# A two-layer backbone kernel: branch products between gate streams, modulation in single matmuls, casts on another engine

## The chip, the cores and the metric

The kernel runs on one core of a Trainium2 chip. The metric is the device time of one execution in microseconds (us), as the median of several runs. The engines are TensorE (PE, with its weight loads listed as PEld), VectorE (DVE), ScalarE (ACT), GpSimd (POOL) and SyncE (SP), which issues the DMAs.

## What is computed

The reference is a backbone of two layers over 512 latent tokens and 256 context tokens of width 1024, in float32. Each layer modulates its normalised input, mixes tokens, passes an MLP, and adds the residual. Cut to the part that the change touches:

```python
mod_l = (silu_c @ w_mod[i] + b_mod[i])           # six sections of 1024: shift, scale, gate, twice
hl = _modulate(xl, sh1_l, sc1_l)
ul_pool, ul_q, ul_k, ul_v, ul_conv, ul_gate = _split_in(hl @ w_in[i] + b_in[i])
ol = _latent_attention(ql, kl, vl, kc, vc, attn_sink[i])     # 8 query heads, 2 key/value heads
# _merge:
y_pool = _pool_mixer(u_pool, pool_w, pool_scale) @ w_pool_out
y_attn = o_attn @ w_attn_out
y_conv = _conv_module(u_conv, conv_w, conv_b, conv_ln_g, conv_ln_b, w_conv_out)
g_pool, g_attn, g_conv = jnp.split(jax.nn.sigmoid(gates), N_BRANCH, axis=-1)
return (g_pool * y_pool + g_attn * y_attn + g_conv * y_conv) @ w_out
```

Context tokens go through the same in layer 0; in layer 1 they serve as keys and values only. The modulation sections 3 and 4 (second shift and scale) of layer 0 are wanted by layer 0's MLP; section 2 is the first gate.

## The kernel before

Float32 products are made of three float32r matmuls each: every operand is split into a high part (a cast to float32r) and a low part (the rest). Weights come by DMA as `raw` tiles of 128x512, ACT casts the high part (L134), POOL or DVE subtracts for the low part (L137), and `mm_a_steps` (L156) issues high x high, high x low and low x high. Where tokens are the moving operand, a stream is 512 columns (latent, LS) or 256 columns (context, CS).

A layer has two phases. `w_phase` makes the input projection, the three mixers, the gates and the branch products; `m_phase` makes the output projection (L165 to L167), the MLP and the next layer's first projections. PE's order is the program's order, written by hand with generators: `drain` runs steps and calls `tick` with each step's columns; `tick` starts tasks that are due (attention blocks, put off by a number of columns with `later`) and, every so many columns, takes one step of a paced generator (`pace`). The instructions of the other engines are ordered by a scheduler, which starts from the program's order.

In `w_phase`, `gated_steps` is the work that covers waits: first the eight attention gates (type 1), then for each of eight output tiles m the pool gate (0) with its branch product and the conv gate (2) with its own. `cover(n)` takes n columns of it while the convolution runs on DVE and while the conv normalisation passes between engines; in the attention stage it is taken step by step between attention tasks. A branch product may be issued only once its input is `mixed`; until then the generator yields None and `cover` returns. `gate_steps` makes one gate: per stream 24 matmuls into a PSUM bank of `psg` (two banks), then a Tanh on ACT (L611). `branch_steps` makes a branch product of 6 matmuls per stream (12 in the last loop) and lets DVE multiply it with the gate (L621). During attention these products take their banks from `psa` (two banks), which the attention's value products (L451, L452) and the conv normalisation use too; afterwards they take them from `psg`.

`mod_steps` makes one modulation section with plain float32 matmuls of a 128x32 stationary operand (L185): for each of eight k, four matmuls with 256 columns each that write to the partitions 0, 32, 64 and 96 of one bank; each matmul is two instructions. In layer 0, section 2 is paced from the start of the phase; sections 3 and 4 are paced from the end of attention on, every 9000 columns, with weight tiles of 512 KB, and what is left of them is issued behind the last branch product (the loop before `pace(None, 0)`).

Queries: `query` evacuates a projection (L665), rotates it (`rope`, L406 to L409), and splits it for each head pair with a cast on DVE (L676) and a subtraction on DVE (L677). Keys: a cast on DVE (L710), a copy on ACT (L711) and two subtractions on DVE (L713) for each of two heads. The second group's queries are made in the middle of the attention.

Of the kernel before, what the change touches and what calls it, by code (L numbers as in the profile page):

```python
# [10 lines left out]
F32 = mybir.dt.float32  # L11
F32R = mybir.dt.float32r
# [6 lines left out]
P = 128  # L19
# [46 lines left out]
ON_C = "G"  # L66
MODVC = ()
W_VAL = 9000
W_CONV0 = 145000
W_CONV1 = 118000  # L70
T_POOL, T_Q, T_K, T_V, T_A, T_B, T_G = 0, 2, 6, 7, 8, 10, 12
# [6 lines left out]
def backbone(ctx: ExitStack, tc: tile.TileContext, I: dict, out: bass.AP):  # L78
# [10 lines left out]
    def uid(s):  # L89
        cnt["n"] += 1  # L90
        return f"{s}_{cnt['n']}"
# [31 lines left out]
    def weight_unit(ap):  # L123
        with tc.high_priority(ring["early"]):
            return weight_parts(ap)
# [47 lines left out]
    def mod_steps(i, s, c0, n, chunk, psum=None, ps=None, row=None):  # L173


        q = n // 4
        ps = bank(psum) if ps is None else ps
        for k in range(KD):
            for j in range(4):
                if j == 0 or (j * q) % w.shape[-1] == 0:  # L180
                    w = chunk()
                    c = c0 + j * q
                    nc.sync.dma_start(out=w, in_=I["wmod"][i, s, k, :, c:c + w.shape[-1]])
                o = (j * q) % w.shape[-1]
                T.matmul(ps[32 * j:32 * j + 32, :q], sc[:, k, :], w[:, o:o + q],  # L185
                         start=(k == 0), stop=(k == KD - 1))
            yield
        mod_finish(i, s, c0, n, ps, row)
        yield
# [221 lines left out]
    def softmax_pv(pp, pss, g, Pt, vtiles, negm, sums, V_, sink, dst, qsl):  # L411
# [26 lines left out]
        for n0 in range(0, nt, 2):  # L438
# [12 lines left out]
                T.matmul(po, w, ph, start=(n == 0), stop=False)  # L451
                T.matmul(po, w, pl, start=False, stop=(n == nt - 1))  # L452
            yield 1024 * len(ns), W_PV
        t1 = pp.tile([64, 4, P], F32, tag="t1", name=uid("t1"), bufs=1)
        S.copy(t1, po[64:128, :].rearrange("p (a q) -> p a q", a=4))
        ot = pp.tile([P, 2, P], F32, tag="ot", name=uid("ot"), bufs=2)
        top = po[0:64, :].rearrange("p (a q) -> p a q", a=4)
        for par in range(2):
            V.tensor_add(ot[64 * par:64 * par + 64, :, :], top[:, par::2, :], t1[:, par::2, :])
# [91 lines left out]
    def pace(steps, every, start=0):  # L551
        pe["pace"], pe["every"], pe["next"] = steps, every, pe["t"] + start
# [7 lines left out]
    def w_phase(i, A, B, has_ctx, pre, todo):  # L560
# [5 lines left out]
        with ExitStack() as ph:  # L566
# [24 lines left out]
            psg = ph.enter_context(tc.tile_pool(name=f"psg{i}", bufs=2, space=PSUM, reuse_waits="tile"))  # L591
            pss = mix.enter_context(tc.tile_pool(name=f"pss{i}", bufs=2, space=PSUM, reuse_waits="tile"))
            if todo:
                pace((x for s in todo for x in mod_steps(i, s, 0, D, lambda: mg.tile(
                    [P, W], F32, tag="sg", name=uid("wm"))[:, :512])), 10000, 20000)

            def proj(t, sls):
# [2 lines left out]
                drain(mm_a_steps(w, A, range(KD), o))  # L600
                return [x[0] for x in o]

            def gate_steps(m, b):

                t = KD * b + m
                w = weight_a(I["win"][i, T_G + t])
                g = mg.tile([P, W], F32, tag="sg", name=uid("sg"))
                for _, sl in outs_all:
                    ps = bank(psg)[:, :sl.stop - sl.start]
                    yield from mm_a_steps(w, A, range(KD), [(ps, sl)])  # L610
                    S.activation(g[:, sl], ps, AF.Tanh, bias=bg[:, t:t + 1], scale=0.5)  # L611
                return g

            def branch_steps(w, ks, w0, g, outs, pool):

                while ks[0] not in mixed:
                    yield None
                for _, sl in outs:
                    ps = bank(pool)[:, :sl.stop - sl.start]
                    yield from mm_a_steps(w, B, ks, [(ps, sl)], w0)  # L620
                    V.scalar_tensor_tensor(out=g[:, sl], in0=g[:, sl], scalar=1.0, in1=ps,  # L621
                                           op0=ALU.add, op1=ALU.mult)

            def gated_steps():
                for m in range(KD):
                    g = yield from gate_steps(m, 1)
                    nc.sync.dma_start(out=sgd[m], in_=g)

                w, d, e, ahead = {}, {}, {}, 0 if todo else 2
                for m in range(ahead):  # L630
                    d[m] = yield from gate_steps(m, 0)
                for m in range(KD + 1):
                    if m + ahead < KD:
                        d[m + ahead] = yield from gate_steps(m + ahead, 0)
                    if m < KD:
                        w[m] = weight_a(I["wbr"][i, m][:, 0:4 * P])
                        yield from branch_steps(w[m], (0, 1), 0, d[m], outs_all, side["bank"])
                    if m:
                        e = yield from gate_steps(m - 1, 2)
                        yield from branch_steps(w.pop(m - 1), (2, 3), 2, e, outs_all, side["bank"])  # L640
                        G.tensor_tensor(out=d[m - 1], in0=d[m - 1], in1=e, op=ALU.add)
                        nc.sync.dma_start(out=mfd[m - 1], in_=d.pop(m - 1))

            mixed, side = set(), {"bank": psa}
            other = gated_steps()

            def cover(cols):
# [20 lines left out]
            def query(Q, g, jj, temp):  # L668
                t = T_Q + 2 * g + jj
                qf = evac(proj(t, LC), t)  # L670
                rope(temp, qf, cs)
                for par in range(2):
                    r = slice(64 * par, 64 * par + 64)
                    ro = slice(64 - 64 * par, 128 - 64 * par)
                    q = Q[2 * jj + par]
                    V.tensor_copy(q[r, :W], qf[r, :W])  # L676
                    V.tensor_tensor(out=q[ro, :W], in0=qf[r, :W], in1=q[r, :W].bitcast(F32),  # L677
                                    op=ALU.subtract)

# [139 lines left out]
            ring["on"] = "GV"  # L819

            fin = ph.enter_context(tc.tile_pool(name=f"fin{i}", bufs=3, reuse_waits="tile"))
            side["bank"] = psg
            if todo:
                pace((x for s in (3, 4) for x in mod_steps(i, s, 0, D, lambda: fin.tile(
                    [P, D], F32, tag="wm", name=uid("wm"), bufs=4))), 9000)
            drain(other)
            for m in range(KD):
                w = weight_a(I["wbr"][i, m][:, 4 * P:8 * P])
# [5 lines left out]
                V.tensor_add(d, d, g)  # L834
                split(A[0][:, m, :W], A[1][:, m, :W], d[:, :], S, G)
            if todo:
                for _ in pe["pace"]:
                    pass
            pace(None, 0)

# [228 lines left out]
    with tc.manual_schedule(engines={mybir.EngineType.PE}):  # L1069
# [159 lines left out]
```

## Time and profile before

| | |
|---|---|
| median of 3 runs | 1978.15 us (1974.14 to 1978.68) |
| profiled execution | 1975.67 us, span from first to last instruction 1973.9 us |
| PE busy | 1848.6 us, 94% of the span |
| DVE, ACT, POOL busy | 1200.3 us (61%), 730.8 us (37%), 771.6 us (39%) |
| mean granted TensorE clock | 0.978 |
| DMA | 244.94 MB, mean 124 GB/s |

Busy time of an engine is the union of its instructions' spans. A row of the timeline gives start, duration, engine, line, operation, operands, and, in brackets, idle time before it with what ended that idle time. Matmuls are pipelined: the time that one takes from its neighbours is read from start to start, not from its duration. In layer 0, `w_phase` runs from about 60 to 543 us of the span, its attention from about 243 to 477; in layer 1 the attention lies at about 1353 to 1527.

### The profile page before, as it was taken

The numbers are of one execution on the slowest core, as the hardware profiler recorded it, in microseconds if no ns is written. First come the engines' busy times: TensorE is split into PE (matmuls) and PEld (weight loads), VectorE is DVE, ScalarE is ACT, GpSimd is POOL, SyncE is SP. The second block draws the span as 40 slices with busy tenths as digits, with TensorE's granted clock in tenths as the row PEclk, the third lists the DMA queues.
The fourth block names the chain that finished last, engine by engine and source line by source line (L and its number), as shares of the span: only waits on it lengthen the run. The fifth ranks groups of instructions, "written<-read, shape, count | busy, mean of one in ns | idle before, by whom it ended". The sixth has DMA issues, their size and how long they took to land. (4 is left out here: it accounts for less than half of the span.)

```text
span 1973.9 us, 27007 instructions
## 1 busy us (share of the span) xinstructions
PE 1848.6 (94%) x9910; PEld 1548.4 (78%) x9910; DVE 1200.3 (61%) x2067; ACT 730.8 (37%) x1359; POOL 771.6 (39%) x629
## 2 busy tenths in 40 slices
PE   6999899899899999999999988999988989999997
PEld 4788788787678888888788868777866768888886
DVE  6489655654478946865533584786575784333356
ACT  4432255353234422233133344434444354333331
POOL 3653432322434422222122546664342554333343
PEclk8999999999999999999999989999999989999999
DMA  8523111114865434464422423141212753332341
GB/s 304 176 90 118 62 59 46 53 44 154 281 219 190 161 112 133 155 213 143 146 62 86 129 96 105 61 149 63 69 65 96 260 189 118 96 96 86 107 129 43
DMA packets 117557, 244.94 MB, mean 124 GB/s; under 512 B 14608, under 2 KB 16944, under 8 KB 117424
## 3 DMA queue, kind: packets, MB, share of 16 engines
q1 hardware_dynamic: 117424, 243.21, 38.0%
q8 instruction: 78, 1.28, 0.3%
q14 instruction: 55, 0.45, 0.1%
HBM read 223.20 MB, written 19.96 MB: 123 GB/s over the span
## 5 line engine op out<-in xcount | busy, mean ns | idle before, releaser
L137 POOL TENSOR_TENSOR wl<-raw,wh 128x512 fp32r<-128x512 f32 x371 | 516.7, 1405 | 783.6 <-ACT wh L134 698.9
L134 ACT CAST wh<-raw 128x512 fp32r<-128x512 f32 x506 | 310.8, 621 | 596.0 <-PE ps L167 292.1
L156 PE MATMUL ps<-actbh,wh 128*128 128x512 f32 (+1 forms) x1016 | 353.4, 348 | 14.3 <-DVE sg L621 6.9
L156 PE MATMUL ps<-actbl,wh 128*128 128x512 f32 (+1 forms) x1016 | 348.3, 343 | 3.1 <-POOL actbl L251 3.1
L156 PE MATMUL ps<-actbh,wl 128*128 128x512 f32 (+1 forms) x1016 | 347.8, 342 | 2.7 <-DVE rs L261 1.3
L156 PE MATMUL ps<-actah,wh 128*128 128x512 f32 (+1 forms) x928 | 331.4, 357 | 13.7 <-ACT actah L248 4.7
L156 PE MATMUL ps<-actal,wh 128*128 128x512 f32 (+1 forms) x928 | 327.4, 353 | 3.3 <-DVE actal L1097 1.9
L156 PE MATMUL ps<-actah,wl 128*128 128x512 f32 (+1 forms) x928 | 326.9, 352 | 0.4 <-POOL wl L137 0.3
L156 PEld LDWEIGHTS ps<-actbh,wh 128*128 128x128 f32 x1016 | 194.5, 191 | 45.2 <-DVE sg L621 10.0
L156 PEld LDWEIGHTS ps<-actbh,wl 128*128 128x128 f32 x1016 | 194.4, 191 | 25.6 <-DVE wl L137 2.4
L156 PEld LDWEIGHTS ps<-actbl,wh 128*128 128x128 f32 x1016 | 194.6, 192 | 23.3 <-POOL actbl L251 3.8
L156 PEld LDWEIGHTS ps<-actah,wh 128*128 128x128 f32 x928 | 177.5, 191 | 43.8 <-ACT actah L248 5.1
L156 PEld LDWEIGHTS ps<-actal,wh 128*128 128x128 f32 x928 | 177.6, 191 | 25.6 <-DVE actal L1097 2.2
L156 PEld LDWEIGHTS ps<-actah,wl 128*128 128x128 f32 x928 | 177.4, 191 | 24.2 <-POOL wl L137 1.0
L165 PE MATMUL ps<-wh,actah 128*128 128x512 f32 x480 | 192.6, 401 | 2.2 <-DVE acc L977 2.0
L167 PE MATMUL ps<-wh,actal 128*128 128x512 f32 x480 | 190.5, 397 | 3.5 <-DVE actal L251 3.5
L166 PE MATMUL ps<-wl,actah 128*128 128x512 f32 x480 | 190.1, 396 | 0.0
L137 DVE TENSOR_TENSOR wl<-raw,wh 128x512 fp32r<-128x512 f32 x135 | 127.8, 947 | 99.9 <-ACT wh L134 97.3
L204 DVE SCALAR_TENSOR_TENSOR wm<-wm,sc,wm 128x512 f32<-128x512 f32 x140 | 124.4, 924 | 67.1 <-DMA wm<-in_wmod 67.0
L970 DVE TENSOR_TENSOR acc<-ps,acc 128x512 f32<-128x512 f32 x140 | 94.7, 684 | 95.3 <-PE ps L167 95.2
L165 PE MATMUL ps<-wh,actbh 128*128 128x512 f32 (+1 forms) x328 | 127.2, 388 | 1.5 <-DVE fg L621 1.5
L166 PE MATMUL ps<-wl,actbh 128*128 128x512 f32 (+1 forms) x328 | 126.8, 387 | 1.0 <-POOL wl L137 1.0
(207 smaller groups left out, 2721.7 us busy)
## 6 DMA issues: line engine op xcount, KB each, us to landing
raw<-in_w SPq DMA_DIRECT2D x264, 256.0 KB
raw<-in_win SPq DMA_DIRECT2D x154, 256.0 KB
wm<-in_wmod SPq DMA_DIRECT2D x72, 512.0 KB
raw<-in_wout SPq DMA_DIRECT2D x56, 256.0 KB
wm<-in_wmod SPq DMA_DIRECT2D x48, 256.0 KB
raw<-in_wbr SPq DMA_DIRECT2D x32, 256.0 KB
x1d<-R SPq DMA_DIRECT2D x10, 512.0 KB
acc<-in_b SPq DMA_DIRECT2D x10, 512.0 KB
```

Of the source, the lines that this page charges most:

```text
L134: S.copy(wh, r)
L137: e.tensor_tensor(out=wl, in0=r, in1=wh[:].bitcast(F32), op=ALU.subtract)
L156: T.matmul(ps, w(hl, w0 + n), x[xi][:, k, sl], start=(start and first and hl == 0 and xi == 0), stop=(stop and last and hl == 1))
L165: T.matmul(ps, x[0][:, k0 + k, tsl], wh, start=(k == 0), stop=False)
L166: T.matmul(ps, x[0][:, k0 + k, tsl], wl, start=False, stop=False)
L167: T.matmul(ps, x[1][:, k0 + k, tsl], wh, start=False, stop=(k == n - 1))
L204: V.scalar_tensor_tensor(out=o, in0=x, scalar=sc[:, k, r:r + 1], in1=o, op0=ALU.mult, op1=ALU.add)
L970: V.tensor_add(a, ps, a)
```

## The change

- Branch products are no longer issued behind both streams of a gate. `gate_steps` puts them on a list (`pend`), and the next gate takes one from the list after each of its streams. All of them use `psg`. The type-0 gates that ran ahead in layer 1 (`ahead` = 2) no longer do.
- Sections 3 and 4 are paced from the start of layer 0's attention, every 3500 columns, with weight tiles of 256 columns (128 KB, three buffers); `mod_steps` then yields after each of the four matmuls of a k. Their PSUM bank comes from `psa`. The pacing behind the attention is gone.
- The casts of queries and of the keys' first copy go from DVE to ACT; the second copy of a key's low part is an ACT copy in place of a DVE subtraction.
- `t1` takes a buffer of `pth`, and `ot` has one buffer in place of two, which makes room for the weight pieces.

The diff, cut to its core:

```diff
+EV_MOD = 3500
@@ mod_steps
                 T.matmul(ps[32 * j:32 * j + 32, :q], sc[:, k, :], w[:, o:o + q],
                          start=(k == 0), stop=(k == KD - 1))
+                if w.shape[-1] == q and j < 3:
+                    yield
             yield
@@ softmax_pv
-        t1 = pp.tile([64, 4, P], F32, tag="t1", name=uid("t1"), bufs=1)
+        t1 = pp.tile([P, 512], F32R, tag="pth", name=uid("pth"), bufs=2)[0:64, :].bitcast(F32)
+        t1 = t1.rearrange("p (a q) -> p a q", a=4)
-        ot = pp.tile([P, 2, P], F32, tag="ot", name=uid("ot"), bufs=2)
+        ot = pp.tile([P, 2, P], F32, tag="ot", name=uid("ot"), bufs=1)
@@ w_phase
-                pace((x for s in todo for x in mod_steps(...)), 10000, 20000)
+                pace((x for s in todo[:1] for x in mod_steps(...)), 10000, 20000)
@@ gate_steps, per stream
                     S.activation(g[:, sl], ps, AF.Tanh, bias=bg[:, t:t + 1], scale=0.5)
+                    if pend:
+                        yield from pend.pop(0)
+                if w2:
+                    pend.extend(piece(w2, ks, ks[0], g, o, done if o is outs_all[-1] else None)
+                                for o in outs_all)
+            def piece(w, ks, w0, g, o, done):
                 while ks[0] not in mixed:
                     yield None
+                yield from branch_steps(w, ks, w0, g, [o], psg)
+                if done:
+                    done(g)
@@ gated_steps
-                w, d, e, ahead = {}, {}, {}, 0 if todo else 2
-                for m in range(ahead):
-                    d[m] = yield from gate_steps(m, 0)
                 for m in range(KD + 1):
-                    if m + ahead < KD:
-                        d[m + ahead] = yield from gate_steps(m + ahead, 0)
                     if m < KD:
-                        w[m] = weight_a(I["wbr"][i, m][:, 0:4 * P])
-                        yield from branch_steps(w[m], (0, 1), 0, d[m], outs_all, side["bank"])
+                        w[m] = weight_half(m)
+                        d[m] = yield from gate_steps(m, 0, w[m], (0, 1))
                     if m:
-                        e = yield from gate_steps(m - 1, 2)
-                        yield from branch_steps(w.pop(m - 1), (2, 3), 2, e, outs_all, side["bank"])
+                        yield from gate_steps(m - 1, 2, w.pop(m - 1), (2, 3), lambda e, m=m: merge(m - 1, e))
+                while pend:
+                    yield from pend.pop(0)
@@ query
-                    V.tensor_copy(q[r, :W], qf[r, :W])
+                    S.copy(q[r, :W], qf[r, :W])
@@ keys
-                V.tensor_copy(KH[g][r, :], kf[r, :])
-                S.copy(KH[g][64 - 64 * g:128 - 64 * g, :], kf[r, :])
-                for r2 in (0, 64):
-                    V.tensor_tensor(out=KL[g][r2:r2 + 64, :], in0=kf[r, :],
-                                    in1=KH[g][r, :].bitcast(F32), op=ALU.subtract)
+                r2 = slice(64 - 64 * g, 128 - 64 * g)
+                S.copy(KH[g][r, :], kf[r, :])
+                S.copy(KH[g][r2, :], kf[r, :])
+                V.tensor_tensor(out=KL[g][r, :], in0=kf[r, :], in1=KH[g][r, :].bitcast(F32), op=ALU.subtract)
+                S.copy(KL[g][r2, :], KL[g][r, :].bitcast(F32))
@@ before the attention
+            if todo:
+                for _ in pe["pace"]:
+                    pass
+                pace((x for s in todo[1:] for x in mod_steps(i, s, 0, D, lambda: pp.tile(
+                    [P, 256], F32, tag="wm", name=uid("wm"), bufs=3))), EV_MOD)
@@ behind the attention
-            side["bank"] = psg
-            if todo:
-                pace((x for s in (3, 4) for x in mod_steps(i, s, 0, D, lambda: fin.tile(
-                    [P, D], F32, tag="wm", name=uid("wm"), bufs=4))), 9000)
@@ layers
-            w_phase(i, A, B, not last, pre, () if i else (2,))
+            w_phase(i, A, B, not last, pre, () if i else (2, 3, 4))
```

## Rows read from the trace of the kernel before

**Rows 1.** The page, part 1: busy us (share of the span) xinstructions.

```profile
PE 1848.6 (94%) x9910; PEld 1548.4 (78%) x9910; DVE 1200.3 (61%) x2067; ACT 730.8 (37%) x1359; POOL 771.6 (39%) x629
```

**Rows 2.** Stages: length, busy us (x) by engine, granted clock, DMA share, GB/s.

```profile
238.00:477.00 239.00, 226.39 (x1351) 196.04 (x1349) 138.61 (x285) 112.51 (x245) 70.28 (x58) 0.99 0.16 51
477.00:543.20 66.20, 57.07 (x387) 41.90 (x388) 26.49 (x37) 17.04 (x26) 30.07 (x19) 0.97 0.86 296
```

**Rows 3.** Waits of PE, 212 to 238 us: total us, times, longest.

```profile
PE ps L156 <- DVE sg L621: 2.9, 2, 2.5
PE ps L734 <- DVE pwh L250: 2.4, 1, 2.4
```

**Rows 4.** Waits of PE, 238 to 477 us (layer 0's attention).

```profile
PE ps L156 <- DVE sg L621: 4.0, 6, 1.4
PE S L501 <- ACT P L515: 3.4, 1, 3.4
PE ps L156 <- ACT qf L665: 2.6, 3, 1.0
...
PE ps L156 <- DVE ot L459: 0.4, 1, 0.4
```

**Rows 5.** Waits of PE, 1255 to 1556 us (layer 1's mixing phase).

```profile
PE S L501 <- DVE q L677: 5.5, 1, 5.5
...
PE ps L452 <- DVE ptl L446: 2.7, 7, 0.8
...
PE ps L156 <- DVE sg L621: 2.0, 1, 2.0
...
PE ps L165 <- DVE fg L621: 1.5, 1, 1.5
```

**Rows 6.** Timeline of PE around one modulation group: start us, us.

```profile
498.76 0.39 PE L156 MATMUL ps<-actbh,wl 128*128 128x512 f32 x1
499.08 0.64 PE L185 MATMUL ps<-wm,sc 128*32 128x256 f32 x8
499.65 0.50 PE L156 MATMUL ps<-actbh,wh 128*128 128x512 f32 x1
```

**Rows 7.** Timeline of PE, the first group behind the attention.

```profile
478.63 0.64 PE L185 MATMUL ps<-wm,sc 128*32 128x256 f32 x8 [1.75 <-DMA wm<-in_wmod]
```

**Rows 8.** Timeline of PE between the last branch product and the next phase.

```profile
532.86 1.50 PE L185 MATMUL ps<-wm,sc 128*32 128x256 f32 x24
...
542.90 0.69 PE L234 MATMUL ps<-ident,row 128*128 128x128 f32 x2 [0.55 <-DVE row L222]
543.24 0.78 PE L165 MATMUL ps<-wh,actah 128*128 128x512 f32 x1
```

**Rows 9.** Timeline of all engines there: the last m's add and low part.

```profile
533.82 2.55 DVE L834 TENSOR_TENSOR fd<-fd,fg 128x768 f32<-128x768 f32 x1
...
537.31 1.82 POOL L251 TENSOR_TENSOR actal<-fd,actah 128x768 fp32r<-128x768 f32 x1 [1.76 <-ACT actah L248]
```

**Rows 10.** Two stretches at the lower clock, columns as in rows 2.

```profile
375.70:379.20 3.50, 3.50 (x13) 2.92 (x12) 1.13 (x3) 1.43 (x4) 1.90 (x2) 0.51 0.00 0
539.60:546.40 6.80, 4.58 (x18) 3.03 (x19) 1.83 (x4) 0.00 (x0) 1.98 (x2) 0.50 0.82 287
```

**Rows 11.** Groups of PE, 477 to 543 us: count | busy us, mean ns | idle before.

```profile
L185 PE MATMUL ps<-wm,sc 128*32 128x256 f32 x128 | 10.3, 404 | 7.4 <-DMA wm<-in_wmod 7.4
```

**Rows 12.** Timeline of PE: the last matmuls of a context stream of a gate.

```profile
203.65 0.28 PE L156 MATMUL ps<-actal,wh 128*128 128x256 f32 x1
203.77 0.28 PE L156 MATMUL ps<-actah,wl 128*128 128x256 f32 x1
```

**Rows 13.** Timeline of SP: the first loads of sections 3 and 4.

```profile
474.52 1.38 SPq L183 DMA_DIRECT2D wm<-in_wmod  x3
```

**Rows 14.** Timeline of ACT: the Tanh of the stream in rows 12.

```profile
204.54 0.47 ACT L611 ACTIVATE sg<-ps,bg 128x256 f32<-128x256 f32 x1
```

**Rows 15.** Timeline of DVE: splitting a query of the second group.

```profile
368.19 2.61 DVE L676 CAST q<-qf 64x768 fp32r<-64x768 f32 x2
370.83 2.88 DVE L677 TENSOR_TENSOR q<-qf,q 64x768 fp32r<-64x768 f32 x2
```

More of the change, by code (lines that the diff above doesn't have):

```diff
@@ L593, in w_phase @@
             if todo:
-                pace((x for s in todo for x in mod_steps(i, s, 0, D, lambda: mg.tile(
+                pace((x for s in todo[:1] for x in mod_steps(i, s, 0, D, lambda: mg.tile(
                     [P, W], F32, tag="sg", name=uid("wm"))[:, :512])), 10000, 20000)
@@ L601, in proj, with gate_steps @@
                 return [x[0] for x in o]
-            def gate_steps(m, b):
+            pend = []
+            def gate_steps(m, b, w2=None, ks=(), done=None):
                 t = KD * b + m
@@ L611, in gate_steps, with branch_steps @@
                     S.activation(g[:, sl], ps, AF.Tanh, bias=bg[:, t:t + 1], scale=0.5)
+                    if pend:
[3 more added lines that the diff above has]
+                                for o in outs_all)
                 return g
-            def branch_steps(w, ks, w0, g, outs, pool):
+            def piece(w, ks, w0, g, o, done):
                 while ks[0] not in mixed:
                     yield None
+                yield from branch_steps(w, ks, w0, g, [o], psg)
+                if done:
+                    done(g)
+            def branch_steps(w, ks, w0, g, outs, pool):
                 for _, sl in outs:
@@ L627, in gated_steps, with merge, weight_half @@
                     nc.sync.dma_start(out=sgd[m], in_=g)
-                w, d, e, ahead = {}, {}, {}, 0 if todo else 2
-                for m in range(ahead):
-                    d[m] = yield from gate_steps(m, 0)
+                w, d = {}, {}
+                def merge(m, e):
+                    G.tensor_tensor(out=d[m], in0=d[m], in1=e, op=ALU.add)
+                    nc.sync.dma_start(out=mfd[m], in_=d.pop(m))
                 for m in range(KD + 1):
-                    if m + ahead < KD:
-                        d[m + ahead] = yield from gate_steps(m + ahead, 0)
                     if m < KD:
-                        w[m] = weight_a(I["wbr"][i, m][:, 0:4 * P])
-                        yield from branch_steps(w[m], (0, 1), 0, d[m], outs_all, side["bank"])
+                        w[m] = weight_half(m)
+                        d[m] = yield from gate_steps(m, 0, w[m], (0, 1))
                     if m:
-                        e = yield from gate_steps(m - 1, 2)
-                        yield from branch_steps(w.pop(m - 1), (2, 3), 2, e, outs_all, side["bank"])
-                        G.tensor_tensor(out=d[m - 1], in0=d[m - 1], in1=e, op=ALU.add)
-                        nc.sync.dma_start(out=mfd[m - 1], in_=d.pop(m - 1))
-            mixed, side = set(), {"bank": psa}
+                        yield from gate_steps(m - 1, 2, w.pop(m - 1), (2, 3), lambda e, m=m: merge(m - 1, e))
+                while pend:
+                    yield from pend.pop(0)
+            def weight_half(m):
+                w = weight_unit(I["wbr"][i, m][:, 0:4 * P])
+                return lambda hl, k: w[hl][:, k * P:(k + 1) * P]
+            mixed = set()
             other = gated_steps()
@@ L836, in w_phase @@
             if todo:
-                for _ in pe["pace"]:
+                for _ in pe["pace"] or ():
                     pass
```

## The prediction

> **What bounds the kernel now.** I read the page's busy line first. TensorE (PE) is busy 94% of the span [rows 1], so an edit pays only by taking work from PE or by ending one of its waits. Then the table by stage, for layer 0's mixing phase, where most of the edit lies: in the attention stage PE is busy 226.4 of 239 us, and in the stage behind it 57.1 of 66.2 us while the DMA engines are at 0.86 [rows 2]. So PE has little idle time during attention and more behind it. Third, PE's own waits by releaser, stage by stage [rows 3 to 5]: these are the prices of what the change can take away. Last, the PE timeline around the modulation matmuls of L185 [rows 6 to 9], which shows what a step of them costs and where PE waits for their weights.
>
> The profiled execution took 1975.67 us, with a span of 1973.9; the median of the runs, 1978.15, lies 2.5 above it. The sum is made against 1975.7.
>
> **The change part by part.**
>
> *Sections 3 and 4 leave the end of layer 0's phase.* There they are 16 steps of four matmuls (eight instructions). Ten stand alone in the stream of L156. The stream's matmul starts at 498.76, the group at 499.08, the next stream matmul at 499.65: 0.89 us from one to the other where 0.23 is usual, so 0.66 is lost [rows 6], and 10 x 0.66 = 6.6. The first of them waited 1.75 for its load [rows 7]. The other six stand behind the last branch product, where PE goes from load to load: from 532.86 to the first matmul of the next phase at 543.24 are 10.4 us [rows 8]. What is late next is the activation of the last m: its add starts at 533.82 and its low half is done at 537.31 + 1.82 = 539.1 [rows 9], which is 6.3 after 532.86. The next phase needs it as its eighth k, for the third matmul, after (7 x 3 + 2) x 0.227 = 5.2; so 1.1 stays, and another 1.5 by the row of layer 1, where this border is crossed without modulation (L165 waits for DVE's fg) [rows 5]. Saved: 10.4 - 2.6 = 7.8. In 539.6 to 546.4 the granted clock was 0.50, the 1.2 GHz level [rows 10], behind these waits; 3.2 us of the next phase ran in it, and 1.6 come back. Sum of this part: 6.6 + 1.75 + 7.8 + 1.6 = **-17.8**.
>
> *They enter the attention as 64 single matmuls.* With 256-column pieces the generator yields after each j, so a piece (two instructions) stands alone in another stream every 3500 columns. By the nearest row four pieces together cost 0.66. Their instructions overlap: 128 of them with a mean of 404 ns fill only 10.3 us [rows 11]. If one alone lasts as long as four (less the stagger of a few ns each), a piece costs 0.64. The other bound: two instructions at the pace of the stream's 256-column matmuls, 0.12 from start to start [rows 12], plus what the group costs beside its two passes. The passes are 0.43 (a run of 24 instructions took 1.50 us, one of 8 took 0.64, 0.43 for each further 8 [rows 6, 8]), which leaves 0.23: 0.24 + 0.23 = 0.47. I take 0.64, since the group is the only row with this shape and its four matmuls are plainly concurrent: 64 x 0.64 = **+41.0** (0.47: 30.1). On PE nothing hides it but PE's own waits, which I count where they are. The Trainium skill, in TensorEngine Tiling (Array Packing), section Tiling Modes, says that column tiles work independently and in parallel, and that a change of tiling mode drains the engine; this speaks against single pieces. By that rule a piece costs 0.64, as in my sum; no run here shows one alone yet.
>
> Each section also ends in two transposes that wait for DVE's row, 0.55 [rows 8]: twice, **+1.1**. The loads (64 of 128 KB on SP, three buffers) I cost at nothing: the three of 512 KB issued from 474.52 on served a matmul at 478.63, at most 4.1 us later [rows 7, 13], and three pieces of 3500 columns (1.6 us) and 0.64 each are 6.6 us ahead. Without that cover PE waits; that is rival 2. One of the two psa banks holds the section's sums all through, so the next block's value products wait until ACT and DVE have emptied the other; about **+1** (0 to 3), the nearest row being 0.4 for a wait on `ot` [rows 4].
>
> *Branch products go between the gate's streams and use psg.* They then no longer wait for psa: PE's waits for DVE sg L621 are 2.9 before the attention, 4.0 in it, 2.0 in layer 1 [rows 3 to 5]: **-8.9**. What is late next is the Tanh of the gate. Gate stream and product now alternate on two banks, and the context stream's bank must be empty after its own last matmul and six more of 0.12, 0.84 us. A 256-column Tanh ends 1.24 after the start of that last matmul (203.77 to 204.54 + 0.47) [rows 12, 14]; 0.4 is missing, for 16 gates 6.4. An attention task or a piece between them takes some of it away, an ACT that is busy 112.5 of 239 us [rows 2] adds some. I take **+5** (0 to 12) for both layers.
>
> *Query and key casts on ScalarE.* The second group's queries are where this lies on PE's path: in layer 0 PE waits 2.6 for qf L665 and 3.4 for the Exp behind DVE's queue, in which two casts and two subtractions take 2.61 + 2.88 us [rows 4, 15]; and 375.7 to 379.2 ran at 0.51 of the clock, 1.7 lost [rows 10]. The casts leave DVE, and some ten pieces of 0.64 fall in this stretch; of 7.7 I let 6 go. In layer 1 PE waits 5.5 for the second query itself [rows 5]; cast, subtraction, cast, subtraction become cast and two subtractions, so 1 goes. **-7** together (4 to 9). What is queued behind on ACT are weight casts and Exps, 0.8 us later at each cast. The keys come while PE is covered by gate streams: 0. The 2.4 us wait on pwh before the attention [rows 3] may go with DVE's shorter queue; I leave it, and keep 4 (with its clock) for the range.
>
> *Layer 1 loses its two gates ahead.* Of its plain streams 10 x 12288 = 122880 columns come before the first one that is blocked on `mixed`, instead of 135168. The pool products want cover up to 118000 + 11200, so 6320 columns, 2.8 us, are missing there. They are streamed later, at the attention's uncovered end, where PE waits 2.7 for ptl in layer 1 [rows 5]. 0, between -2 and +4.
>
> `t1` in a `pth` buffer and a single `ot`: consumers are done within a block, 0.
>
> Sum: 41.0 + 1.1 + 1 + 5 - 17.8 - 8.9 - 7 = **+14.4**, so 1990.1 against the profiled execution, 1992.6 against the median. I give 1991.
>
> **The rivals.**
> 1. *Not slower: a piece alone is cheap.* Place: the 64 L185 matmuls in attention. Without them the sum is 7.1 - 33.7 = -26.6, so the change breaks even at 26.6 / 64 = 0.42 a piece. At 0.24, two passes at the stream's pace and no cost of switching, it is 15.4 - 26.6 = -11.2: 1965. For it: PE's waits in attention could swallow switching. Against: the group's row, which shows 0.23 beside its passes.
> 2. *The pieces' loads come late.* SP issues in order, and raw weight loads that wait for buffers stand before them. For it: PE has waited for these loads before [rows 7, 8]. Against: it did so only where the issue was late. At 0.3 a piece, 19 more: 2010.
> 3. *It cancels.* A piece costs the lower bound of 0.47: 30.1 - 26.6 = +3.5, 1979; or the Tanh waits don't come (-5) and pwh goes (-4).
> 4. *It doesn't do what it says*: products that still wait on a bank, -8.9 not gained. It ends where rival 2 does and has no chance of its own.
>
> **How the numbers follow.** Forecast (1983 to 2003) 0.55; rival 1 0.17; rival 2 0.08; rival 3 0.20. A measurement can tell about 0.3%, 6 us, from no change. Faster is rival 1, 0.17; same is rival 3, 0.20; slower is the forecast and rival 2, 0.63. The range goes from 1966, which is rival 1 at 0.26 a piece, to 2006, which is the forecast with the Tanh, psa and layer 1 waits at their upper ends (+7, +2, +4) and a piece at 0.66; about 0.16 lies outside.
>
> **What would show it.** L185 in the attention as 128 instructions in pairs, with about 0.87 us from the stream matmul before to the one behind a pair: this decides between the forecast and rivals 1 and 3. No L185 behind 532, and the border of the phases without the 10 us. No PE wait for DVE sg L621, but waits of PE for ACT sg L611 behind 256-column streams. The second query's wait in layer 0 almost gone. Rival 2 would show as PE waits for wm in attention. The prediction is wrong if pairs cost under 0.5, or if PE's waits in attention fall by far more than the 10 us I count there.

## The result, and the profile after

The kernel after takes 2002.25 us (median of 4 runs, 2000.57 to 2006.79), beside 1976.14 for the kernel before (4 runs, 1971.34 to 1978.68): a ratio of 1.0139, with a 95% interval of 1.0111 to 1.0166. It is slower, as forecast, and inside the range, but by 26 us and not by 14. Its profiled execution took 2001.27 us with a span of 1999.3, so against the profiled execution of before the rise is 25.6.

Lines have shifted. In the trace of after, the gate streams are L157 (L156 before), the modulation matmuls L186 (L185), the gate's Tanh L618 (L611), the product with the gate L638 (L621), the evacuation of a projection L686 (L665), the query's cast and subtraction L697 and L698 (L676, L677), the rotation L409 to L412 (L406 to L409).

The page of after, part 1, the line that answers [rows 1]:

```profile
PE 1882.5 (94%) x9910; PEld 1558.4 (78%) x9910; DVE 1173.4 (59%) x2042; ACT 749.5 (37%) x1383; POOL 766.9 (38%) x630
```

PE has the same 9910 instructions and is busy 33.9 us longer; its idle time falls from 125.3 to 116.8. So on balance the extra time is dearer work and not more waiting. The balance hides two new waits, though; the next table tells where both lie.

It gives the time between PE's first instructions of a kind, in us of the span: vt are the transposes of the values (about 104 in layer 0), "products" the pool mixer's matmuls (204), "score" the attention's first (245), "PV" its last value product (474), "wout" the output projection's first (543). Columns from e1 on are the experiments below; differences in the text are made before rounding.

| stretch | before | after | e1 | e2 | e3 | e4 | e5 | e7 | e8 | e9 |
|---|---|---|---|---|---|---|---|---|---|---|
| start to vt, layer 0 | 104.1 | 102.8 | 104.8 | 101.3 | 103.6 | 102.7 | 101.7 | 103.7 | 102.6 | 101.6 |
| vt to products | 100.5 | 109.1 | 100.5 | 109.0 | 100.5 | 100.5 | 108.8 | 100.5 | 100.5 | 100.5 |
| products to score | 40.0 | 34.9 | 34.5 | 34.5 | 34.8 | 34.3 | 37.5 | 37.6 | 35.9 | 34.7 |
| attention, score to PV | 229.6 | 268.9 | 267.8 | 245.8 | 241.4 | 235.8 | 224.3 | 229.2 | 240.6 | 234.7 |
| PV to wout | 69.1 | 47.8 | 47.8 | 47.8 | 48.5 | 48.5 | 70.3 | 69.0 | 48.6 | 47.8 |
| wout to vt of layer 1 | 705.2 | 708.1 | 707.8 | 710.0 | 709.1 | 705.5 | 706.9 | 706.7 | 709.0 | 712.3 |
| vt to products, layer 1 | 76.3 | 85.2 | 75.0 | 85.8 | 75.0 | 75.0 | 85.2 | 76.2 | 76.3 | 75.0 |
| products to score, layer 1 | 28.4 | 26.1 | 26.2 | 28.2 | 26.1 | 26.1 | 28.0 | 29.6 | 29.6 | 25.8 |
| attention, layer 1 | 171.9 | 167.0 | 171.2 | 166.4 | 171.3 | 168.8 | 172.8 | 173.2 | 173.2 | 169.7 |
| PV to wout, layer 1 | 25.3 | 26.4 | 25.4 | 25.0 | 25.2 | 25.6 | 25.7 | 25.9 | 26.0 | 25.7 |
| wout to the end | 423.6 | 423.1 | 423.6 | 424.1 | 424.2 | 423.1 | 424.0 | 423.1 | 423.2 | 422.8 |

From before to after four stretches move by more than 6 us: layer 0's attention +39.4, what is behind it -21.3, and, twice, vt to products, +8.6 and +9.0. (The next is products to score in layer 0, -5.1.) The first two are the change that the sum worked out. The two stretches from vt to products it priced at nothing.

The windows of after, columns as in [rows 2]: the attention, and what is behind it.

```profile
246.00:515.90 269.90, 263.98 (x1445) 200.22 (x1444) 131.05 (x270) 115.50 (x247) 68.15 (x55) 0.99 0.24 75
515.90:563.40 47.50, 47.19 (x271) 41.38 (x270) 22.96 (x36) 14.35 (x22) 27.58 (x16) 1.00 0.78 262
```

PE now idles 5.9 us in the attention and 0.3 behind it, where the stages of [rows 2] had 12.6 and 9.1. PE's waits in the attention of after (total us, times, longest), which answer [rows 4]:

```profile
PE ps L157 <- ACT qf L686: 2.0, 3, 1.0
PE ps L186 <- DMA wm<-in_wmod: 1.8, 1, 1.8
PE ps L157 <- DVE sg L638: 0.9, 2, 0.5
PE ps L157 <- ACT sg L618: 0.8, 2, 0.6
```

The wait for DVE's product is down from 4.0 to 0.9, the Exp's 3.4 is gone, and the Tanh, for which +5 was allowed in both layers, costs 0.8 here. The loads of the pieces cost 1.8, once.

The timeline of PE around one lone piece in the attention, and the group of L186 between 246 and 450 us (count | busy us, mean ns | idle before), which answer [rows 6] and [rows 11]:

```profile
285.95 0.40 PE L455 MATMUL ps<-ptl,V 128*128 128x512 f32 x1
286.27 0.62 PE L186 MATMUL ps<-wm,sc 128*32 128x256 f32 x2
286.82 0.50 PE L157 MATMUL ps<-actah,wh 128*128 128x512 f32 x1
...
L186 PE MATMUL ps<-wm,sc 128*32 128x256 f32 x128 | 39.9, 393 | 1.8 <-DMA wm<-in_wmod 1.8
```

From the matmul before the piece to the one behind it are 0.87 us, the very figure that was to decide; less the 0.23 of the matmul itself, a lone piece takes 0.64. The same 128 instructions that filled 10.3 us in groups of eight [rows 11] now fill 39.9.

The border of the phases, which answers [rows 8]:

```profile
563.32 0.28 PE L157 MATMUL ps<-actbh,wl 128*128 128x256 f32 x1
563.44 0.40 PE L166 MATMUL ps<-wh,actah 128*128 128x512 f32 x1
563.67 0.40 PE L167 MATMUL ps<-wl,actah 128*128 128x512 f32 x1
```

The 10.4 us from load to load are gone, without a wait in their place at this border.

Now the stretches that were priced at nothing. PE's waits before the attention (105 to 246 us), and below them those of layer 1's mixing phase, which answer [rows 3] and [rows 5]:

```profile
PE ps L157 <- ACT sg L618: 6.1, 1, 6.1
PE ps L354 <- DVE cn L348: 2.3, 3, 1.5
PE ps L755 <- DVE pwh L253: 1.1, 1, 1.1
...
PE ps L157 <- ACT sg L618: 8.0, 1, 8.0
PE ps L455 <- DVE ptl L449: 3.3, 5, 1.8
...
PE S L505 <- DVE q L698: 1.5, 2, 1.2
```

Both new waits are for a Tanh (L618), one of 6.1 us in layer 0 and one of 8.0 in layer 1, each a single event. A Tanh takes 0.69 us. What kept ACT from it is in ACT's timeline (136 to 151 us, then layer 1):

```profile
136.44 0.47 ACT L686 ACTIVATE qf<-ps,b_in 128x256 f32<-128x256 f32 x1
147.99 1.69 ACT L697 CAST q<-qf 64x768 fp32r<-64x768 f32 x2 [11.09 <-DVE qf L412]
149.70 0.69 ACT L618 ACTIVATE sg<-ps,bg 128x512 f32<-128x512 f32 x1
150.29 1.13 ACT L135 CAST wh<-raw 128x512 fp32r<-128x512 f32 x2
...
1310.08 1.26 ACT L697 CAST q<-qf 64x512 fp32r<-64x512 f32 x2 [13.67 <-DVE qf L412]
1311.36 0.69 ACT L618 ACTIVATE sg<-ps,bg 128x512 f32<-128x512 f32 x1
```

ACT evacuates the projection of the first group's second query, and its next instruction is that query's cast. The cast waits 11.1 us (13.7 in layer 1) for DVE to finish the rotation, and the Tanh and the weight casts, which are behind the cast in ACT's order, wait with it. The Trainium skill, in Trainium Architecture — The Big Picture, section Inside one NeuronCore, says that each engine has its own instruction stream and that engines meet only through semaphores; the trace agrees, with 11.1 us in which ACT ran nothing. The Tanh behind the cast was due in the second half of them: PE's last matmul before its wait starts at 144.05, and in e1 below, without the cast, the same Tanh starts 5.1 us after that evacuation, which would be 141.5 here. Why the rotation is late is in DVE's timeline of the same stretch:

```profile
137.17 2.41 DVE L400 SCALAR_TENSOR_TENSOR pd<-pw,up 64x256 f32<-64x256 f32 x2
...
142.98 0.75 DVE L409 STREAM_SHUFFLE rt<-qf 128x512 f32<-128x512 f32 x1
...
146.17 1.73 DVE L412 TENSOR_TENSOR qf<-qf,rt 128x512 f32<-128x512 f32 x1 [0.49 <-POOL rt L410]
```

The projection was evacuated at 136.9 (136.44 + 0.47), but DVE was still at the pool mixer (L400) and the convolution (L326), began the rotation at 142.98 and ended it at 147.90. Behind each of the two waits PE also ran slowly: the windows of the two stretches, columns as in [rows 2].

```profile
148.40:155.20 6.80, 4.76 (x11) 3.80 (x12) 6.71 (x13) 3.34 (x6) 2.52 (x2) 0.50 0.37 125
1308.90:1315.70 6.80, 3.60 (x9) 2.82 (x10) 6.56 (x10) 4.05 (x7) 4.61 (x5) 0.50 0.34 104
```

The granted clock was 0.50, the 1.2 GHz level, in both. In the first PE was busy 4.76 us, with work that is about half as long at the full clock (in the second stretch the stream's matmuls start 0.43 apart, where 0.23 is usual), so 2.4 us are lost; 6.1 + 2.4 = 8.5, and the stretch is 8.6 longer. In layer 1, 8.0 + 3.60 / 2 = 9.8, less the 1.3 that the key edits give there (e8 below), is 8.5, and it is 9.0 longer.

### The profile page after: what moved, and what is told of

It reads as the page before. It is cut to its first block, busy times and chain, and to the rows that moved or that the text cites. A ratio compares the mean times of both kernels' runs of the same rounds, so it can differ in the third digit from the quotient of the medians.

```text
span 1999.3 us, 27079 instructions
## 1 busy us (share of the span) xinstructions
PE 1882.5 (94%) x9910; PEld 1558.4 (78%) x9910; DVE 1173.4 (59%) x2042; ACT 749.5 (37%) x1383; POOL 766.9 (38%) x630
## 3 DMA queue, kind: packets, MB, share of 16 engines
q1 hardware_dynamic: 124336, 243.21, 37.6%
## 5 line engine op out<-in xcount | busy, mean ns | idle before, releaser
L157 PE MATMUL ps<-actbh,wh 128*128 128x512 f32 (+1 forms) x1016 | 354.4, 349 | 12.7 <-ACT sg L618 8.3
L157 PE MATMUL ps<-actah,wh 128*128 128x512 f32 (+1 forms) x928 | 337.6, 364 | 18.5 <-ACT sg L618 6.9
L157 PE MATMUL ps<-actbl,wh 128*128 128x512 f32 (+1 forms) x1016 | 350.3, 345 | 4.7 <-POOL actbl L254 4.6
L157 PE MATMUL ps<-actbh,wl 128*128 128x512 f32 (+1 forms) x1016 | 349.4, 344 | 2.7 <-DVE rs L264 1.3
L157 PE MATMUL ps<-actal,wh 128*128 128x512 f32 (+1 forms) x928 | 327.9, 353 | 4.1 <-DVE actal L1120 2.1
L157 PE MATMUL ps<-actah,wl 128*128 128x512 f32 (+1 forms) x928 | 327.4, 353 | 0.4 <-POOL wl L138 0.3
L157 PEld LDWEIGHTS ps<-actah,wh 128*128 128x128 f32 x928 | 177.5, 191 | 68.8 <-issue 25.5
L157 PEld LDWEIGHTS ps<-actbh,wh 128*128 128x128 f32 x1016 | 196.6, 193 | 41.3 <-issue 9.4
L157 PEld LDWEIGHTS ps<-actbl,wh 128*128 128x128 f32 x1016 | 196.7, 194 | 25.4 <-POOL actbl L254 5.4
L157 PEld LDWEIGHTS ps<-actbh,wl 128*128 128x128 f32 x1016 | 196.5, 193 | 25.5 <-DVE wl L138 2.4
L157 PEld LDWEIGHTS ps<-actal,wh 128*128 128x128 f32 x928 | 177.7, 192 | 26.2 <-POOL actal L254 3.1
L157 PEld LDWEIGHTS ps<-actah,wl 128*128 128x128 f32 x928 | 177.5, 191 | 24.6 <-POOL wl L138 1.1
```

The costliest lines, as they stand in the source:

```text
L157: T.matmul(ps, w(hl, w0 + n), x[xi][:, k, sl], start=(start and first and hl == 0 and xi == 0), stop=(stop and last and hl == 1))
```

## The experiments

Two theories stood against each other first. By the one, the lone pieces cost what the sum says, and what is missing in it is the query's cast in ACT's order. By its rival the casts are harmless, and the pieces and the products between the streams cost more than the sum says through what surrounds them.

### e1: the query's cast back on DVE

```diff
-                    S.copy(q[r, :W], qf[r, :W])
+                    V.tensor_copy(q[r, :W], qf[r, :W])
```

> The changed kernel with the query casts back on DVE (all groups, both layers); key copies stay on ACT. Theory A: the casts of the first group's second query hold ACT's queue (idle 11.1 and 13.7 us in front of them, behind DVE's rotation), and with it the Tanh and the weight casts; PE then waits 6.1 and 8.0 us, and each wait is followed by 6.8 us at the lower clock (3.4 lost each). Undone: -21, less up to 5 that the second group's queries gave: 1981 to 1987 us, and no PE wait for the gate's Tanh before the pool products in either layer. Rival: the key copies on ACT or the products between the streams make these waits; then they stay and the time is 1999 to 2005.

Measured: 1986.16 us (4 runs, 1985.86 to 1988.94) against 1976.99, a ratio of 1.0064 (1.0047 to 1.0081). PE's waits between 105 and 245 us:

```profile
PE ps L354 <- DVE cn L348: 2.4, 3, 1.5
PE ps L186 <- DMA wm<-in_wmod: 1.9, 1, 1.9
PE ps L755 <- DVE pwh L253: 0.6, 1, 0.6
```

No Tanh is waited for, because ACT now makes it as soon as PE's stream is done, as its timeline shows:

```profile
143.55 0.69 ACT L618 ACTIVATE sg<-ps,bg 128x512 f32<-128x512 f32 x1 [4.59 <-PE ps L157]
```

vt to products is back at 100.5 and 75.0 us. One edit gives 16.1 us by the medians and 14.7 by the profiled spans; the two stretches give 18.8, and layer 1's attention loses 4.2, since the second group's casts have gone back too. So the first theory holds for the two stretches. The kernel is still 9 us slower than before (10.7 by the spans): +38.2 in the attention and -21.3 behind it, less 6.2 in the other stretches, 5.5 of them between products and score in layer 0.

### e2: modulation pieces in pairs

```diff
-EV_MOD = 3500
+EV_MOD = 7000
-                if w.shape[-1] == q and j < 3:
+                if w.shape[-1] == q and j == 1:
```

> The changed kernel with modulation pieces in pairs: the generator yields after j = 1 and 3 in place of every j, and is paced every 7000 columns in place of 3500. Theory A (four, two or one cost the same on PE, 0.64 to 0.65 us for a visit): 32 visits x 0.65 in place of 64 x 0.64, so -20: 1980 to 1985. Rival: the attention grew by the bank that the sums hold and by Tanh waits, and single pieces lie in time that PE would wait anyway; then within 5 us of 2002.

Measured: 1980.6 us (7 runs, 1976.21 to 1987.89), a ratio of 1.0022 (0.9999 to 1.0045). PE's timeline around one pair, and the group of L186 in the attention:

```profile
303.57 0.28 PE L513 MATMUL S<-kl,q 128*128 128x256 f32 x1
303.78 0.63 PE L186 MATMUL ps<-wm,sc 128*32 128x256 f32 x4
304.33 0.39 PE L157 MATMUL ps<-actah,wh 128*128 128x256 f32 x1
...
L186 PE MATMUL ps<-wm,sc 128*32 128x256 f32 x128 | 20.4, 391 | 1.9 <-DMA wm<-in_wmod 1.9
```

Two matmuls together take what one took alone: 303.57 to 304.33 is 0.76, less the 0.12 of a 256-column matmul 0.64. They are 32 steps now in place of 64, and the attention is 23.1 us shorter (268.9 to 245.8), where 32 x 0.64 is 20.5; the other 2.6 aren't allotted. The two waits for a Tanh are not touched by this edit, and vt to products stays at 109.0 and 85.8. The price hangs on the number of steps, not on the work in them.

### e3: groups of four, with the query's cast on DVE

The generator doesn't yield inside a k any more; the pace keeps the same columns in all. Four weight buffers in place of three are paid with a query's scratch tile, which moves to a tag that has room.

```diff
-EV_MOD = 3500
+EV_MOD = 14000
-                if w.shape[-1] == q and j < 3:
-                    yield
-                    S.copy(q[r, :W], qf[r, :W])
+                    V.tensor_copy(q[r, :W], qf[r, :W])
-                    [P, 256], F32, tag="wm", name=uid("wm"), bufs=3))), EV_MOD)
+                    [P, 256], F32, tag="wm", name=uid("wm"), bufs=4))), EV_MOD)
-    query(Q, g, jj, pp.tile([P, TL], F32, tag="rt", name=uid("rt"), bufs=1))
+    query(Q, g, jj, pp.tile([P, 512], F32R, tag="ptl", name=uid("ptl"), bufs=2).bitcast(F32))
```

> The changed kernel with modulation steps of four matmuls (no yield between them, paced every 14000 columns, four buffers; to make room the rotation's scratch tile of the second group takes a ptl buffer) and with the query casts back on DVE. Theory A: 16 visits x 0.66 = 10.6 in place of 41.0, so -30, and -16 to -21 as in the run with the casts undone alone: 1950 to 1958, about 20 us under the kernel before. Rival (the two effects overlap, since PE waits elsewhere when it gets through sooner): 1965 to 1975.

Measured: 1959.94 us (4 runs, 1957.85 to 1967.73), a ratio of 0.9934 (0.9911 to 0.9958): faster than before, though by 2 us less than was expected at the least. From e1 to e3 the attention falls by 26.4 us (267.8 to 241.4) for 48 steps fewer, 0.55 a step where the sum says 0.64, or 4.3 us less in all. Most of that is one wait of PE, which e1, with lone pieces in that stretch, doesn't have. It shows in the timelines of DVE, ACT and PE:

```profile
373.87 2.62 DVE L695 CAST q<-qf 64x768 fp32r<-64x768 f32 x2
376.51 2.91 DVE L696 TENSOR_TENSOR q<-qf,q 64x768 fp32r<-64x768 f32 x2
379.63 0.69 ACT L517 ACTIVATE P<-S,ngm 128x512 f32<-128x512 f32 x1 [3.40 <-DVE ngm L514]
380.82 0.73 PE L157 MATMUL ps<-actah,wh 128*128 128x512 f32 x1 [3.66 <-ACT sg L616]
```

The cast and the subtraction of the second query hold DVE until 379.42. The Exp needs a result of DVE (ngm) that comes behind them, a Tanh stands behind the Exp on ACT, and PE waits 3.7 us for that Tanh. The window from the first score to the end of the attention, columns as in [rows 2]:

```profile
238.90:480.50 241.60, 230.85 (x1440) 193.62 (x1439) 136.34 (x272) 111.22 (x242) 68.91 (x55) 0.99 0.27 84
```

PE idles 10.8 us in it, against 6.2 in the attention of e1.

### e7: the products between the streams, and nothing else

Before, with only the hunks of `pend`, `piece` and `gated_steps`; modulation and casts are as before.

> The kernel before with the branch products between the next gate's streams, and nothing else of the change (modulation as before, casts as before, t1 and ot as before). My sum: -8.9 of waits for DVE sg L621, + 3 to 5 of Tanh waits: 1970 to 1974 where the kernel before has 1976. Rival: the Tanh waits and the missing cover in layer 1 eat all of it: 1976 to 1982.

Measured: 1976.43 us (10 runs, 1973.19 to 1978.93), a ratio of 1.0 (0.9988 to 1.0013). The gain that was expected didn't come; it is the rival's 1976. The forecast had -8.9 and +5 for this part. PE's waits in its attention, and its longest:

```profile
PE ps L157 <- DVE sg L637: 5.4, 3, 4.1
PE ps L157 <- ACT qf L685: 2.6, 3, 1.0
PE ps L157 <- ACT sg L617: 1.2, 2, 0.6
...
371.82 0.50 PE L157 MATMUL ps<-actah,wh 128*128 128x512 f32 x1 [4.14 <-DVE sg L637]
```

The wait for DVE's product didn't go, it moved: a gate stream now waits for a bank of `psg` that a product holds until DVE has multiplied it, and DVE is at the second group's query: in DVE's timeline the cast and the subtraction fill 365.15 to 370.67, and the multiplication starts at 371.36. It was 4.0 in six events [rows 4] and is 5.4 in three. Layer 0 gains 2.8 us from products to the end of the attention, layer 1 loses 2.6 there; whether that loss is of the products or of the two gates that no longer run ahead isn't separated. In after this wait is 0.9. That is not the work of the casts alone: in e1, with the same casts on DVE and lone pieces in the stream, it is 1.1. In e3 and e8, with few steps and the casts on DVE, one wait of 3.7 us for a Tanh comes behind the same cast and subtraction (see e3).

### e5: the casts, and nothing else

Before, with only the query's cast and the keys' copies moved to ACT.

> The kernel before with the query and key casts on ACT and nothing else of the change. Theory A (the first group's query casts hold ACT's queue): PE waits about 6 and 8 us for Tanh before the pool products of the two layers and loses some 3.4 to the clock behind each, and the second group gives back 4 to 8: net +10 to +16, 1986 to 1992. Rival (only together with the new order of the gates does a held ACT reach PE): within 4 of the kernel before, 1973 to 1981.

Measured: 1988.15 us (10 runs, 1983.18 to 1995.93), a ratio of 1.0057 (1.0037 to 1.0078). PE's waits before the attention, and in layer 1 between 1250 and 1340 us:

```profile
PE ps L156 <- ACT sg L611: 6.1, 1, 6.1
...
PE ps L156 <- ACT sg L611: 8.0, 1, 8.0
```

The same two waits of the same size come without any other part of the change. So they don't need the products between the streams or the pieces: the cast in ACT's order is enough. The keys' copies, which this run moves too, are not what makes them, since e1 keeps those on ACT and has no such wait. In the attention of layer 0 these casts are worth 5.2 us: the Exp's 3.4 [rows 4] and the 1.7 that the lower clock behind it took [rows 10] are gone, while the 2.6 for qf stay. In layer 1's attention they give nothing here (172.8 against 171.9).

### e8: e3 with the keys' casts as before

```diff
-                S.copy(KH[g][r, :], kf[r, :])
-                S.copy(KH[g][r2, :], kf[r, :])
-                V.tensor_tensor(out=KL[g][r, :], in0=kf[r, :], in1=KH[g][r, :].bitcast(F32), op=ALU.subtract)
-                S.copy(KL[g][r2, :], KL[g][r, :].bitcast(F32))
+                V.tensor_copy(KH[g][r, :], kf[r, :])
+                S.copy(KH[g][64 - 64 * g:128 - 64 * g, :], kf[r, :])
+                for r2 in (0, 64):
+                    V.tensor_tensor(out=KL[g][r2:r2 + 64, :], in0=kf[r, :],
+                                    in1=KH[g][r, :].bitcast(F32), op=ALU.subtract)
```

> The changed kernel with modulation in steps of four (as in the run that was fastest so far) and with every cast of queries and keys back on DVE: what the moved products and the moved sections give by themselves. Against the run with the key casts on ACT (1960) it shows what the keys are worth. Theory: keys on ACT shorten DVE's queue before the pool products by about 3 us per layer, which PE sees as 1 to 3 each: 1960 to 1966. Rival: the key casts cost as the query casts do, since ACT waits for DVE's rotation there too: 1952 to 1958.

Measured: 1966.75 us (7 runs, 1963.8 to 1968.82), a ratio of 0.9943 (0.9922 to 0.9963), 6.8 above e3 by the medians and 5.9 by the spans. The ratios of the two (0.9943 and 0.9934) have intervals that overlap, so this total is not settled. The stretches say more. e3 is shorter than e8 by 1.1 us between products and score in layer 0, and in layer 1 by 1.3, 3.5 and 1.9 in the three stretches from vt to the last PV; in layer 1, e1 agrees with e3, and e7, which has no key casts on ACT either, with e8. So the keys' casts on ACT are a gain, which the sum put at 0; the ratios put it at 1.8 us, the medians at 6.8. One wait differs plainly: that of PE for the pool mixer's low weight part in layer 1, of e8 and then of e3.

```profile
PE ps L755 <- POOL pwl L252: 2.1, 1, 2.1
```

```profile
PE ps L755 <- POOL pwl L252: 0.8, 1, 0.8
```

It is 1.3 of the 3.5 between products and score; the rest isn't allotted.

### e4: e3 with the second group's query cast on ACT

```diff
-                    V.tensor_copy(q[r, :W], qf[r, :W])
+                    if g:
+                        S.copy(q[r, :W], qf[r, :W])
+                    else:
+                        V.tensor_copy(q[r, :W], qf[r, :W])
```

> Modulation in steps of four; query casts on DVE for the first group, on ACT for the second (in the attention); key casts on ACT. Theory: in the attention no long DVE chain stands ahead of the rotation, so the casts there give layer 1 about 4 us (its attention was 4.2 longer with all query casts on DVE) and layer 0 up to 3: 1952 to 1957. Rival: ACT is what the attention waits for, and it stays at 1960 or goes over it.

Measured: 1950.92 us (4 runs, 1948.45 to 1955.87), a ratio of 0.9863 (0.9833 to 0.9894). This beats both kernels: 26 us under before (1976.9 beside it), 51 under after. Its waits before the attention, the second query's cast on ACT in it, one of the steps of four, and their group:

```profile
PE ps L352 <- DVE cn L346: 2.3, 3, 1.5
PE ps L186 <- DMA wm<-in_wmod: 1.6, 1, 1.6
...
371.52 1.69 ACT L696 CAST q<-qf 64x768 fp32r<-64x768 f32 x2 [0.41 <-DVE qf L410]
...
299.27 0.28 PE L157 MATMUL ps<-actbh,wl 128*128 128x256 f32 x1
299.48 0.64 PE L186 MATMUL ps<-wm,sc 128*32 128x256 f32 x8
300.05 0.38 PE L157 MATMUL ps<-actbh,wh 128*128 128x256 f32 x1
...
L186 PE MATMUL ps<-wm,sc 128*32 128x256 f32 x128 | 11.7, 391 | 1.6 <-DMA wm<-in_wmod 1.6
```

A step of four takes 0.78 - 0.12 = 0.66. Of the 11.7 us the first step has 2.08, because its four pieces land one after another: its weight loads wait another 1.1 us for them. With the casts of the second group alone, no Tanh is waited for ahead of the attention, and layer 0's attention is 5.6 us shorter than in e3, layer 1's 2.5. Of the 5.6, 3.5 are the wait that e3 shows at 380.82: here it is 0.2, at 375.47, and the cast stands only 0.41 us on ACT for its input. So ACT is the right engine for these casts in the attention, where PE waits behind DVE's queue, and the wrong one in the first group, where their input is late and a Tanh stands behind them.

### e9: e4 with the first modulation step later

The first step of a section comes 7000 columns later, to give its load time.

```diff
-                    [P, 256], F32, tag="wm", name=uid("wm"), bufs=4))), EV_MOD)
+                    [P, 256], F32, tag="wm", name=uid("wm"), bufs=4))), EV_MOD, 7000)
```

> As the run with only the second group's casts on ACT, with the first modulation step 7000 columns (3 us) after the start of the attention in place of at once. Theory: the wait of 1.8 us for the first weight pieces and the lower clock behind it go: 2 to 3 us under that run. Rival: the loads stand behind others on SP and are late wherever the first step is: no difference.

Measured: 1951.27 us (4 runs, 1949.75 to 1958.07), a ratio of 0.9869 (0.9837 to 0.99). The wait of 1.6 for the load is gone, and from the first vt to wout e9's profile is 1.5 us shorter than e4's. But the time is that of e4: 712.3 us from wout to vt of layer 1, where e4 has 705.5, hide any gain. That stretch lies behind the attention. In it the kernels that issue the modulation inside the attention run the same code, and they differ by up to 7 us; a term of 2 us can't be read from one profile of them.

## Why the prediction was right, and where it was wrong

**Right: the lone piece.** 0.64 was taken, against a bound of 0.47; it is 0.64 (285.95 to 286.82 less 0.23). 64 of them are the change's main cost, and e2 and e4 show the same price for two (0.64) and for four matmuls (0.66). The Trainium skill's rule that was weighed there (TensorEngine Tiling (Array Packing), section Tiling Modes: tiles work in parallel, a change of mode drains the engine) agrees with 39.9, 20.4 and 11.7 us for the same 128 instructions in 64, 32 and 16 steps. Rival 1, which needed under 0.42, falls with it, and so does the first case of rival 3. The second case of rival 3 came in large part: the Tanh waits of the gates that it left out are small, and pwh went from 2.4 to 1.1.

**Right in the sum: the attention and its end.** The terms of layer 0's attention were 41.0 + 1.1 + 1 + 5 - 4.0 - 6 = 38.1, with the Tanh term, given for both layers, put here whole; measured are 39.4. Single terms in it differ: the Tanh waits are 0.8 there and 0.2 or none elsewhere outside the two long ones, the product waits fell by 3.1 and not 4.0. The query's casts, put at -6, are worth 5.2 in e5, but nothing between e1 and after: e1, with the casts on DVE, is even 1.1 shorter there, and the Exp's wait is gone in it too. And 2.6 of the 7.7 us that the prediction laid to DVE's queue, the wait for qf, don't hang on the casts: e5 still has them. So that the sum comes within 1.3 us is in part luck, of misses that cancel. Behind the attention -17.8 was forecast and -21.3 measured; 2.6 of the 3.5 more are the waits that the sum left at the border of the phases and that did not come, and the rest isn't allotted.

**Right: rival 2 doesn't come.** PE waits for a piece's load once, 1.8 us, where the rival wanted 19.

**Wrong: the step on the casts.** It said "What is queued behind on ACT are weight casts and Exps, 0.8 us later at each cast. The keys come while PE is covered by gate streams: 0." Two things failed. It priced the cast's duration on ACT, not the time for which the cast waits there for its own input, and it looked only at the second group's queries, in the attention. In the first group the rotation stands behind the pool mixer and the convolution on DVE, so ACT stands still for 11.1 and 13.7 us, a Tanh is due behind it, and PE waits 6.1 and 8.0 us and then runs 4.8 and 3.6 us at the lower clock. Forecast 0, measured +8.6 and +9.0; e1 takes both away, and e5 makes both alone.

**The gap, and luck.** The gap between forecast and result is 25.6 - 14.4 = 11.2. It is +17.6 from this step, +1.3 in layer 0's attention, -3.5 behind it, -2.2 between products and score of layer 0 (-5.1 for -2.9), -3.1 in layer 1 from products to wout (-6.1 for -3), and +1.1 in the three other stretches. So the rest of the sum was too high by 6.4, and that hides a third of the step that failed. That 2002 still lies in the range is luck in this sense: the range's upper end was made of Tanh, psa and layer 1 waits, none of which came in that size, and a term that the range did not have took their place.

**Wrong in size: the products.** -8.9 for the waits on DVE, +5 for the Tanh; alone the part gives nothing (e7). In e7 the longest wait on DVE is one for DVE's queue, so another bank moves it and doesn't end it. Before the attention the gain is there (products to score 40.0 to 37.6), in layer 0's attention it is 0.4 us, and in layer 1 it is a loss. In after the waits on DVE for a product are 0.9 in all, where before had 8.9, but there the order of PE's work has changed too.

**Wrong in size: the keys, and layer 1.** The keys' casts were put at 0 and are a gain (e8 to e3, 6.8 us by the medians, its size not settled). The second group's queries in layer 1 (-1 forecast) give 4.2 us of its attention between e1 and after. These gains cover part of the step that failed. e5, with the same casts and the old order of the gates, doesn't show the 4.2, so they hang on that order too; why isn't shown.

**Open.** The +2.9 from wout to vt of layer 1 lies within the 7 us by which that stretch differs between e4 and e9. That the products must leave `psa` if the sections are to sit there follows from the code (two banks); it wasn't tried.

## What to carry to other kernels

Before moving an operation to another engine, look up when its input is ready and which instruction stands right behind it there: a cast of 1.7 us cost 8.6, because it was put ahead of a Tanh while its input was 11 us away; the same cast in the attention is worth 5.6. Work that costs by the step (here 0.64, whether it holds one, two or four matmuls) is put between other work in as few steps as the buffers allow. And a wait for an engine whose queue is full doesn't go away with another bank (4.1 us in e7, 3.7 in e3); here it went with work taken out of that queue (0.2 in e4).

## What the runs showed of the hardware

A float32 matmul (two instructions) with a 128x32 stationary operand and 256 columns takes 0.64 us of TensorE when it stands alone between matmuls of the full array, and two or four of them on as many column tiles take 0.64 and 0.66: 64, 32 and 16 steps filled 39.9, 20.4 and 11.7 us (the last with one step of 2.08 whose pieces were still landing). And a single wait of TensorE of 6.1 or 8.0 us was each time followed by work at the 1.2 GHz level: the granted clock fell to 0.50 some 2 or 3 us before the wait ended (148.4 and 1308.9, where PE goes on at 150.44 and 1312.10) and stayed there for 6.8 us.
